# Feed-forward input projections as seven half products, in a hybrid encoder block

## The chip, the cores and the metric

One core of a Trainium2 chip runs the whole layer in one launch. The metric is the device time of the launch in microseconds, and lower is better. The core's engines have their own instruction queues: TensorE (PE in the profile) multiplies matrices into PSUM, VectorE (DVE) and ScalarE (ACT) do elementwise work, GpSimd (POOL) does elementwise work too, and SyncE (SP) starts DMA transfers.

## The reference

512 tokens, model width 1024, all in float32. The layer is: a feed-forward block, a mixer, a second feed-forward block, a final norm.

```python
x = x + 0.5 * swiglu(rms_norm(x, ffn1_norm), ffn1_w_in, ffn1_w_out)
...                      # mixer: h = rms_norm(x); P = h @ w_in; gated convolution, SSD scan, merge
x = x + 0.5 * swiglu(rms_norm(x, ffn2_norm), ffn2_w_in, ffn2_w_out)
return rms_norm(x, final_norm)

def swiglu(h, w_in, w_out):
    g, u = jnp.split(h @ w_in, 2, axis=-1)      # w_in is 1024 x 5632, two halves of 2816
    return (jax.nn.silu(g) * u) @ w_out
```

## The kernel before, in words

**Layout.** The activations are kept transposed: 128 features on the partitions, 512 tokens along the row, so the width of 1024 is 8 tiles (`KT`). The hidden width of 2816 is 22 tiles (`FT`).

**Precision.** A product in float32 is made from three products in the faster type fp32r. Each operand is split into a high part (a cast) and a low part (the rest): `wh`, `wl` for a weight block, and two halves of `xw` for an input. `mm3` (L169) issues for each of the 8 input tiles high x high, high x low and low x high, all into one PSUM bank. So a projection to 128 output features is 24 matmuls that each stream 512 columns.

**Weights.** `prep` (L110) takes the next 512 KB block from the list `src`: SyncE loads it to `wraw` (two buffers), ScalarE casts it to `wh` (L124), VectorE subtracts to get `wl` (L125). `take` (L131) hands out the oldest prepared block and starts the next `prep`; `wh` and `wl` have three buffers each.

**Feed-forward.** `ffn` (L249) loops over the 22 hidden tiles. For each it runs one projection for the gate and one for the up half, and then `hidden` (L253): VectorE multiplies both by the norm's factor per token (`tg`, `tu`), ScalarE takes SiLU (`sg`), GpSimd multiplies (`hf`, L261), and `split` makes the high and low part of the hidden tile (`hk`). Then the output projection runs over 8 output tiles `m`, 22 hidden tiles each, in three weight blocks (`kcut`), and VectorE adds half of the result to the residual (L275). The residual `xall` stays in SBUF through the whole program. In the second feed-forward block the last output tile is done in two halves of 256 tokens, with the final norm and the stores behind them (`finish`, L684).

**Order.** TensorE's instructions stand as the code issues them. `Order` (L42) counts finished input tiles (ticks), and pieces such as the norm's sums are put in when a tick is reached. The other engines' order is made by the scheduler of the tile framework; a tile is written only when its buffer's last users are done.

Of the kernel before, what the change touches and what calls it, by code (L numbers as in the profile page):

```python
# [17 lines left out]
P = 128  # L18
# [21 lines left out]


# [28 lines left out]
def hybrid_block(ctx: ExitStack, tc: tile.TileContext, xT, w1i, w1o, wmx, wz0, wso, wsso,  # L70
# [3 lines left out]
    wp = ctx.enter_context(tc.tile_pool(name="wp", bufs=3))  # L74
    act = ctx.enter_context(tc.tile_pool(name="act", bufs=1))
    tp = ctx.enter_context(tc.tile_pool(name="tp", bufs=2))
    ps = ctx.enter_context(tc.tile_pool(name="ps", bufs=1, space=bass.MemoryType.PSUM))
    ctx.enter_context(tc.manual_schedule(engines={mybir.EngineType.PE}))
# [4 lines left out]
    src += [(w1i[i], KT) for i in range(2 * FT)]  # L83
    kcut = [(0, 8), (8, 16), (16, FT)]
    fout = lambda w: [(w[m, :, a * P : b * P], b - a) for m in range(KT) for a, b in kcut]
# [19 lines left out]
    src += [(w2i[i], KT) for i in range(2 * FT)]  # L105
# [4 lines left out]
    def prep():  # L110

        if not src:
            return
        ap, _ = src.pop(0)
        n = ap.shape[-1]
        raw = wp.tile([P, D], F32, tag="wraw", name="wraw", bufs=2)
        cuts = [slice(0, n)]
        if len(src) >= NSRC - 2:
            cuts = [slice(0, n // 2), slice(n // 2, n)]
        nc.sync.dma_start(raw[:, :n], ap)  # L120
        wh = wp.tile([P, D], F32R, tag="wh", name="wh")
        wl = wp.tile([P, D], F32R, tag="wl", name="wl")
        for h in cuts:
            cast = nc.scalar.copy(wh[:, h], raw[:, h])  # L124
            nc.vector.tensor_tensor(wl[:, h], raw[:, h], wh[:, h].bitcast(F32), ALU.subtract)  # L125
        ready.append((wh, wl))
        return cast

    NSRC = len(src)

    def take():  # L131
        w = ready.pop(0)
        prep()
        return w


    xall = pers.tile([P, KT, T], F32, name="xall")
    xr = [xall[:, j, :] for j in range(KT)]
# [19 lines left out]

    warm = tp.tile([P, NC], F32, tag="ms", name="warm")
# [9 lines left out]
    def mm3(out, w, xs, first=True, last=True, tk=slice(0, T)):  # L169

        wh, wl = w
        n = len(xs)
        for i, xk in enumerate(xs):
            sl = slice(i * P, (i + 1) * P)
            nc.tensor.matmul(out, wh[:, sl], xk[:, 0, tk], start=first and i == 0, stop=False)  # L175
            nc.tensor.matmul(out, wh[:, sl], xk[:, 1, tk], start=False, stop=False)  # L176
            nc.tensor.matmul(out, wl[:, sl], xk[:, 0, tk], start=False, stop=last and i == n - 1)  # L177
            sq.tick()
# [7 lines left out]
    def split(dst, s):  # L186
        nc.scalar.copy(dst[:, 0, :], s)
        nc.vector.tensor_tensor(dst[:, 1, :], s, dst[:, 0, :].bitcast(F32), ALU.subtract)

    class Norm:  # L190
# [3 lines left out]
        def __init__(self, gain):  # L194
# [3 lines left out]
            self.xw = []  # L198

        def parts(self, j):  # L200
            xk = act.tile([P, 2, T], F32R, tag="xw", name="xw", bufs=KT)
            g = col(self.gain + j)
            nc.scalar.activation(xk[:, 0, :], xr[j], AF.Copy, scale=g)  # L203
            nc.vector.scalar_tensor_tensor(xk[:, 1, :], xr[j], g, xk[:, 0, :].bitcast(F32),  # L204
                                           ALU.mult, ALU.subtract)
            self.xw.append(xk)
# [42 lines left out]
    def ffn(nrm, nxt, tags=("mm",)):  # L249
# [3 lines left out]
        def hidden(pg, pu):  # L253
# [7 lines left out]
            nc.gpsimd.tensor_tensor(hf, sg, tu, ALU.mult)  # L261
# [4 lines left out]
        for f in range(FT):  # L266
            pg = project(xw, tags[2 * f] if 2 * f < len(tags) else "mm")
            pu = project(xw, tags[2 * f + 1] if 2 * f + 1 < len(tags) else "mm")
            sq.at(nrm.ok, lambda pg=pg, pu=pu: hidden(pg, pu))
        sq.run()  # L270
        for m in range(KT if nxt is not None else KT - 1):
            pt = bank()
            for a, b in kcut:
                mm3(pt, take(), hid[a:b], a == 0, b == FT)
            nc.vector.scalar_tensor_tensor(xr[m], pt, 0.5, xr[m], ALU.mult, ALU.add)  # L275
# [6 lines left out]
        return hid  # L282


    n1 = Norm(PF_N1)
    prep()
    for j in range(0, KT, 2):
        nc.sync.dma_start(xall[:, j : j + 2, :], xT[:, j : j + 2, :])
    keep(12, "sg", zeros("ta"))
    for j in range(KT):  # L290
        n1.parts(j)
        if j == 6:
            cast = prep()
    nc.sync.dma_start(pf[:, PF_SC:], pfeat[:, PF_SC:])
    nc.sync.dma_start(cst, csts[:, :3, :])
    mgt = tp.tile([P, P], F32, tag="td", name="mgt", bufs=3)
    nc.sync.dma_start(mgt, csts[:, 3, :])
    nc.sync.dma_start(pr, prow)

    def first_sums():  # L300
        with tc.issue_after(cast.ins):
# [3 lines left out]

    sq.at(9, first_sums)
    n1.later(22, 28)
# [475 lines left out]
```

## Time and profile before

| | |
|---|---|
| median of 3 runs | 1499.1 us (1498.96 to 1499.4) |
| profiled execution, its own time | 1499.53 us |
| span of the profiled execution | 1497.7 us |
| TensorE busy | 1486.5 us, 99% of the span |
| VectorE busy | 794.9 us, 53% |
| ScalarE busy | 604.5 us, 40% |
| GpSimd busy | 223.7 us, 15% |
| granted TensorE clock | 0.999 of full speed |
| DMA | 139.49 MB, 93 GB/s in the mean |

How to read it: in a row of the timeline stand start and duration in us, the engine, the line of the kernel, the operation, what it writes and reads, and the shape. Matmuls overlap, so the pace of TensorE is the distance from one start to the next, not the duration. In a row of a group stand count, busy time, mean duration in ns, and the idle time of the engine ahead of the group with its releaser.

### The profile page before, as it was taken

The numbers are of one execution on the slowest core, as the hardware profiler recorded it, in microseconds if no ns is written. First come the engines' busy times: TensorE is split into PE (matmuls) and PEld (weight loads), VectorE is DVE, ScalarE is ACT, GpSimd is POOL, SyncE is SP. The second block draws the span as 40 slices with busy tenths as digits, with TensorE's granted clock in tenths as the row PEclk, the third lists the DMA queues.
The fourth block names the chain that finished last, engine by engine and source line by source line (L and its number), as shares of the span: only waits on it lengthen the run. The fifth ranks groups of instructions, "written<-read, shape, count | busy, mean of one in ns | idle before, by whom it ended". The sixth has DMA issues, their size and how long they took to land.

```text
span 1497.7 us, 18035 instructions
## 1 busy us (share of the span) xinstructions
PE 1486.5 (99%) x7233; PEld 1252.9 (84%) x7234; DVE 794.9 (53%) x925; ACT 604.5 (40%) x914; POOL 223.7 (15%) x206
## 2 busy tenths in 40 slices
PE   9999999999999999999999999999999999999998
PEld 6888888888888999888888888888888888888887
DVE  6454554333687777778653256554544545453223
ACT  6233332222587777667641122222243322232222
POOL 1111111000033322212200011111121111110011
PEclk9999999999999999999999999999999999999999
DMA  5323333323312222122223333333222222223333
GB/s 194 98 86 101 96 99 92 105 89 99 93 63 67 69 77 71 58 85 71 71 81 113 93 94 98 99 99 99 96 100 86 98 99 96 101 86 104 88 106 106
DMA packets 40964, 139.49 MB, mean 93 GB/s; under 512 B 4656, under 2 KB 7088, under 8 KB 40880
## 3 DMA queue, kind: packets, MB, share of 16 engines
q1 hardware_dynamic: 40192, 137.79, 29.6%
q8 instruction: 57, 0.93, 0.3%
q10 hardware_dynamic: 688, 0.54, 0.1%
q14 instruction: 27, 0.22, 0.0%
HBM read 136.22 MB, written 2.10 MB: 92 GB/s over the span
## 4 chain that ended last, share of the span: by engine, by line
PE 96%; DVE 2%; DMA 1%; issue 0%; ACT 0%; POOL 0%; SPq 0%; POOLq 0%; ACTq 0%; DVEq 0%
PE mm L176 28%; PE mm L175 28%; PE mm L177 28%; PE mm L327 2%; PE mm L328 2%; PE mm L326 2%; PE py L514 2%; PE sg L501 1%; DVE cv L392 1%; PE po L525 1%; PE po L469 1%; DVE wl L125 0%; PE sg L425 0%; DMA xall<-xT 0%; PE tr L446 0%
## 5 line engine op out<-in xcount | busy, mean ns | idle before, releaser
L124 ACT CAST wh<-wraw 128x1024 fp32r<-128x1024 f32 (+2 forms) x262 | 269.7, 1030 | 679.4 <-PE mm L176 625.9
L175 PE MATMUL mm<-xw,wh 128*128 128x512 f32 x1256 | 500.4, 398 | 0.5 <-ACT xw L203 0.5
L125 DVE TENSOR_TENSOR wl<-wraw,wh 128x1024 fp32r<-128x1024 f32 (+2 forms) x262 | 386.0, 1474 | 213.0 <-ACT wh L124 211.9
L176 PE MATMUL mm<-xw,wh 128*128 128x512 f32 x1256 | 489.2, 389 | 0.5 <-DVE xw L204 0.5
L177 PE MATMUL mm<-xw,wl 128*128 128x512 f32 x1256 | 489.6, 390 | 0.0
L177 PEld LDWEIGHTS mm<-xw,wl 128*128 128x128 f32 x1256 | 235.7, 188 | 50.0 <-DVE wl L125 0.4
L176 PEld LDWEIGHTS mm<-xw,wh 128*128 128x128 f32 x1256 | 236.1, 188 | 48.4 <-DVE xw L204 1.2
L175 PEld LDWEIGHTS mm<-xw,wh 128*128 128x128 f32 x1256 | 235.9, 188 | 48.3 <-ACT xw L203 1.0
L175 PE MATMUL mm<-hk,wh 128*128 128x512 f32 (+1 forms) x374 | 141.0, 377 | 0.0
L176 PE MATMUL mm<-hk,wh 128*128 128x512 f32 (+1 forms) x374 | 140.8, 377 | 0.0
L177 PE MATMUL mm<-hk,wl 128*128 128x512 f32 (+1 forms) x374 | 140.8, 376 | 0.0
L261 POOL TENSOR_TENSOR hf<-sg,tu 128x512 f32<-128x512 f32 x44 | 59.5, 1353 | 400.5 <-ACT wh L124 285.1
L259 DVE TENSOR_TENSOR tu<-mm,rb 128x512 f32<-128x512 f32 x42 | 29.0, 692 | 134.2 <-PE mm L177 134.2
L177 PEld LDWEIGHTS mm<-hk,wl 128*128 128x128 f32 x374 | 70.4, 188 | 13.0
L176 PEld LDWEIGHTS mm<-hk,wh 128*128 128x128 f32 x374 | 70.4, 188 | 12.9
L175 PEld LDWEIGHTS mm<-hk,wh 128*128 128x128 f32 x374 | 70.4, 188 | 12.8
L392 DVE SCALAR_TENSOR_TENSOR cv<-xp,pf,cv 128x512 f32<-128x512 f32 x96 | 73.9, 769 | 2.6 <-ACT cv L389 1.1
L326 PE MATMUL mm<-wh,xw 128*128 128x256 f32 (+1 forms) x256 | 74.9, 293 | 0.0
L327 PE MATMUL mm<-wl,xw 128*128 128x256 f32 (+1 forms) x256 | 72.7, 284 | 0.0
L328 PE MATMUL mm<-wh,xw 128*128 128x256 f32 (+1 forms) x256 | 72.7, 284 | 0.0
L255 DVE TENSOR_TENSOR tg<-mm,rb 128x512 f32<-128x512 f32 x43 | 29.7, 692 | 66.9 <-PE mm L177 63.3
L216 POOL TENSOR_TENSOR nacc<-nacc,nsq 128x512 f32<-128x512 f32 x18 | 26.4, 1469 | 223.5 <-ACT nsq L213 223.5
(182 smaller groups left out, 1669.9 us busy)
## 6 DMA issues: line engine op xcount, KB each, us to landing
wraw<-wmx SPq DMA_DIRECT2D x86, 512.0 KB, 3.6
wraw<-w1i SPq DMA_DIRECT2D x44, 512.0 KB, 3.6
wraw<-w2i SPq DMA_DIRECT2D x44, 512.0 KB, 3.2
wraw<-w2o SPq DMA_DIRECT2D x18, 512.0 KB, 3.5
wraw<-w1o SPq DMA_DIRECT2D x16, 512.0 KB, 3.5
wraw<-wsso SPq DMA_DIRECT2D x16, 512.0 KB, 3.8
wraw<-wso SPq DMA_DIRECT2D x8, 512.0 KB, 3.2
wraw<-wmo SPq DMA_DIRECT2D x8, 512.0 KB, 3.2
```

The lines of the kernel that those rows point to most:

```text
L124: cast = nc.scalar.copy(wh[:, h], raw[:, h])
L125: nc.vector.tensor_tensor(wl[:, h], raw[:, h], wh[:, h].bitcast(F32), ALU.subtract)
L175: nc.tensor.matmul(out, wh[:, sl], xk[:, 0, tk], start=first and i == 0, stop=False)
L176: nc.tensor.matmul(out, wh[:, sl], xk[:, 1, tk], start=False, stop=False)
L177: nc.tensor.matmul(out, wl[:, sl], xk[:, 0, tk], start=False, stop=last and i == n - 1)
L255: nc.vector.tensor_tensor(tg, pg, nrm.rb, ALU.mult)
L261: nc.gpsimd.tensor_tensor(hf, sg, tu, ALU.mult)
L326: nc.tensor.matmul(o, xw[k][:, 0, tk], wh[:, sl], start=k == 0, stop=False)
L327: nc.tensor.matmul(o, xw[k][:, 0, tk], wl[:, sl], start=False, stop=False)
L328: nc.tensor.matmul(o, xw[k][:, 1, tk], wh[:, sl], start=False, stop=k == KT - 1)
L392: nc.vector.scalar_tensor_tensor(cv, xp[:, q : q + T], col(PF_CW + 4 * ft + q), cv, ALU.mult, ALU.add)
L514: nc.tensor.matmul(py[:, h, :], self.ex[c][:, h, :], self.xdt[:, c, d0 : d0 + P], start=True, stop=True)
```

## The change

**Seven half products.** For a pair (the gate tile and the up tile of one hidden tile) the two weight blocks are seen as a 2 x 2 matrix of blocks: rows are gate and up, columns are the two halves of the input width (4 input tiles each). The input is a 2 x 2 matrix too: rows are the halves of the width, columns are tokens 0 to 255 and 256 to 511. Instead of 8 block products the Strassen form (Winograd's) takes 7, with sums of blocks made ahead on both sides. Each block product is 4 input tiles x 3 fp32r products of 256 columns.

- `Norm.sums_of_x` makes the four sums of the input, once for each block, and their high and low parts (`hT`, `lT`).
- `Pair.prepare` makes the weight side: the gate's parts `gh`, `gl`; the sums `f13`, `f24` and their parts `h13`, `l13`, `h24`, `l24`; the up half's second half `a22`. The gate's low part is not a subtraction on VectorE: ScalarE writes the negated high part into `gl`, and a DMA that GpSimd starts adds the weights from DRAM to it (`accum_op`).
- `Pair.product` issues the 12 matmuls of a product, `Pair.after` the work behind it. The order of products is 1, 5, 4 of the pair before, 6, 2, 3, 7. Products 1, 6, 7 and 4 accumulate in one bank, and its intermediate states are copied out (`p1`, `p6`) or read (`ut`). Two sets of three banks alternate.
- 4 hidden tiles of the first block (`N1`) and 1 of the second (`N2`) stay plain; their projections run while the sums are made. 18 + 21 = 39 tiles go as pairs.
- The factor per token of the up half moves to the output side (`add`), where the residual is updated in two VectorE steps instead of one. The product of gate and up moves from GpSimd to VectorE. `hid` stays float32, and its split to `hk` is done in the output projection, whose first two output tiles therefore run side by side.

**Buffers.** Raw weights have three buffers of their own. All else of that size, prepared weights, inputs, hidden tiles and the residual, shares 38 slots. The residual leaves SBUF: the first block reloads the input `xT` after its pairs, stores the result to DRAM (`xs1`), and the second does so with `xs1` and `xd`. In mixer groups 0 and 1 `prep` is queued on ScalarE behind what was issued there last (`turns`).

**Order, TensorE.** In the middle of the first block's projections; `mm_...` and `py_...` are banks, and `wh`, `wl` the weight's parts. Before, one projection (its first two input tiles):

```order
L175 MATMUL mm_1027<-xw_110,wh_950 128x512
L176 MATMUL mm_1027<-xw_110,wh_950 128x512
L177 MATMUL mm_1027<-xw_110,wl_951 128x512
L175 MATMUL mm_1027<-xw_113,wh_950 128x512
L176 MATMUL mm_1027<-xw_113,wh_950 128x512
L177 MATMUL mm_1027<-xw_113,wl_951 128x512
```

Now, where product 5 of a pair ends and product 4 of the pair before begins:

```order
L433 MATMUL mm_1283<-hT_422,h13_1194 128x256
L433 MATMUL mm_1283<-lT_423,h13_1194 128x256
L433 MATMUL mm_1283<-hT_422,l13_1214 128x256
L433 MATMUL py_1153<-hT_255,a22_1135 128x256
L433 MATMUL py_1153<-lT_256,a22_1135 128x256
L433 MATMUL py_1153<-hT_255,a22_1135 128x256
L433 MATMUL py_1153<-hT_297,a22_1135 128x256
```

The rows stream 256 columns instead of 512, and a bank of the pair before is written once more inside the next pair. Over the program 1872 matmuls of 512 columns go and 3276 of 256 come; all other matmuls keep their number and shape.

**Order, VectorE.** At the same place. Before, in a hidden tile's time:

```order
L259 TENSOR_TENSOR tu_774<-mm_735,rb_297 128x512
L125 TENSOR_TENSOR wl_763<-wraw_760,wh_762 128x1024
L188 TENSOR_TENSOR hk_778<-hf_776,hk_778 128x512
L255 TENSOR_TENSOR tg_843<-mm_766,rb_297 128x512
L125 TENSOR_TENSOR wl_805<-wraw_802,wh_804 128x1024
```

Now, for one pair (`gt`, `ut`, `hid` of the pair on TensorE, the rest for the pair after the next), with `a22_1263` of 512 columns behind it:

```order
L447 TENSOR_TENSOR gt_1116<-mm_1027,p1_1040 128x256
L449 TENSOR_TENSOR gt_1116<-mm_1026,p6_1100 128x256
L450 TENSOR_TENSOR gt_1116<-gt_1116,rb_379 128x512
L456 TENSOR_TENSOR ut_1150<-mm_1025,p5_1061 128x256
L463 TENSOR_TENSOR hid_1024<-ut_1150,gt_1116 128x256
L372 TENSOR_TENSOR f13_1191<-wraw_1102 128x512
L373 TENSOR_TENSOR f13_1191<-wraw_1047,wraw_1102 128x512
L380 TENSOR_TENSOR f24_1209<-wraw_1047,f13_1191 128x512
L381 TENSOR_TENSOR f24_1209<-wraw_1047,f24_1209 128x512
L459 TENSOR_TENSOR hid_1024<-mm_1025,gt_1116 128x256
L388 TENSOR_TENSOR l13_1214<-f13_1191,h13_1194 128x1024
L388 TENSOR_TENSOR l24_1246<-f24_1209,h24_1212 128x1024
```

Five instructions became thirteen. In every second pair the rows of `f13` and `f24` stand between those of `gt` and `ut`.

**Order, ScalarE.** Before, in a hidden tile's time and the start of the next:

```order
L187 CAST hk_778<-hf_776 128x512
L124 CAST wh_804<-wraw_802 128x1024
L257 ACTIVATE sg_845<-tg_843 128x512
L124 CAST wh_835<-wraw_833 128x1024
L187 CAST hk_851<-hf_849 128x512
```

Now (`gl` is what the accumulating DMA waits for):

```order
L451 ACTIVATE gt_1116<-gt_1116 128x512
L357 ACTIVATE gl_1170<-wraw_1047 128x1024
L443 COPY p1_1168<-py_1153 128x256
L359 CAST gh_1172<-wraw_1047 128x1024
L443 COPY p5_1189<-po_1154 128x256
L375 CAST h13_1194<-f13_1191 128x1024
L383 CAST h24_1212<-f24_1209 128x1024
L443 COPY p6_1228<-py_1153 128x256
L394 CAST a22_1263<-wraw_1102 128x512
```

The copies out of the banks stand between the casts of the next weights.

The core of the diff:

```diff
+KH, TH, DH = KT // 2, T // 2, D // 2
+N1, N2 = 4, 1
+RAWS = 3
+SLOTS = 41 - RAWS
...
+        def gate_parts(self, add=True):
+            rg = self.raw[0]
+            self.gl = a4("gl", [P, D], F32R)
+            if add:
+                nc.scalar.activation(self.gl, rg, AF.Copy, scale=-1.0)
+            self.gh = a4("gh", [P, D], F32R)
+            nc.scalar.copy(self.gh, rg)
+            if add:
+                nc.gpsimd.dma_start(self.gl, self.w[2 * self.f], accum_op=ALU.add)
+            else:
+                nc.vector.tensor_tensor(self.gl, rg, self.gh.bitcast(F32), ALU.subtract)
...
+        def s13(self):
+            a11, _ = self.halves(0)
+            a21, a22 = self.halves(1)
+            self.f13 = a4("f13", [P, 2, DH])
+            nc.vector.tensor_tensor(self.f13[:, 0, :], a21, a22, ALU.add)
+            nc.vector.tensor_tensor(self.f13[:, 1, :], a11, a21, ALU.add)
+            self.h13 = a4("h13", [P, 2, DH], F32R)
+            nc.scalar.copy(self.h13, self.f13)
...
+        def product(self, n, nrm):
+            out = {1: self.a, 6: self.a, 7: self.a, 4: self.a, 5: self.c, 3: self.c, 2: self.b}[n]
+            xi = {1: 0, 2: 2, 3: 3, 5: 4, 6: 5, 7: 6, 4: 7}[n]
+            wh, wl = self.weights(n)
+            first = n in (1, 5, 2)
+            for k in range(KH):
+                xh, xl = nrm.form(xi, k)
+                sl = slice(k * P, (k + 1) * P)
+                for i, (wk, xk) in enumerate(((wh, xh), (wh, xl), (wl, xh))):
+                    nc.tensor.matmul(out, wk[:, sl], xk, start=first and k == i == 0,
+                                     stop=k == KH - 1 and i == 2, skip_group_check=True)
...
+        def after(self, n, nrm, hid):
+            lo, hi = slice(0, TH), slice(TH, T)
+            if n in (1, 5, 6):
+                t = tp.tile([P, TH], F32, tag={1: "st0", 5: "st1", 6: "st2"}[n], name="p%d" % n, bufs=1)
+                nc.scalar.copy(t, self.c if n == 5 else self.a)
+                setattr(self, "p%d" % n, t)
+            elif n == 2:
+                self.g = tp.tile([P, T], F32, tag="tc", name="gt")
+                nc.vector.tensor_tensor(self.g[:, lo], self.b, self.p1, ALU.add)
+            elif n == 3:
+                nc.vector.tensor_tensor(self.g[:, hi], self.c, self.p6, ALU.add)
+                nc.vector.tensor_tensor(self.g, self.g, nrm.rb, ALU.mult)
+                nc.scalar.activation(self.g, self.g, AF.Silu)
...
-            tu = tp.tile([P, T], F32, tag="tc", name="tu")
-            nc.vector.tensor_tensor(tu, pu, nrm.rb, ALU.mult)
-            hf = tp.tile([P, T], F32, tag="td", name="hf", bufs=3)
-            nc.gpsimd.tensor_tensor(hf, sg, tu, ALU.mult)
-            hk = act.tile([P, 2, T], F32R, tag="act", name="hk", bufs=FT)
-            split(hk, hf)
-            hid.append(hk)
...
+        for p, q in enumerate(pairs):
+            hid_tile(q.f)
+            q.banks(sets[p % 2])
+            order = (1, 5, 4, 6, 2, 3, 7) if p < len(pairs) - 1 else (1, 5, 4, 6, 2, 7, 3)
+            for step, n in enumerate(order):
+                o = prev if n == 4 else q
+                if o is not None:
+                    o.product(n, nrm)
+                    o.after(n, nrm, hid[o.f])
+                if p or step:
+                    ahead(p + 1, step)
+            prev = q
...
+            nc.vector.scalar_tensor_tensor(t[:, :n], pt, -0.5, nrm.rb[:, tk], ALU.mult, ALU.mult)
+            nc.vector.tensor_tensor(xr[m][:, tk], t[:, :n], xr[m][:, tk], ALU.add)
```

More of the change, by code (lines that the diff above doesn't have):

```diff
@@ L267, in ffn @@
+        hk = []
+        for f in range(plain):
+            hid_tile(f)
             pg = project(xw, tags[2 * f] if 2 * f < len(tags) else "mm")
+            if f == plain - 1:
+                sq.at(sq.now + 4, lambda: ahead(1, 0))
             pu = project(xw, tags[2 * f + 1] if 2 * f + 1 < len(tags) else "mm")
[L269 to L275, printed above, removed]
+            sq.at(nrm.ok, lambda f=f, pg=pg, pu=pu: hidden(f, pg, pu))
@@ L292, in hybrid_block @@
         if j == 6:
[L293 to L298, printed above, removed]
+            prep(halves=True)
     def first_sums():
-        with tc.issue_after(cast.ins):
+        with behind():
             for j in range(KT):
```

357 lines of the change are left out of this document (283 added, 74 removed).

## The prediction

> **What bounds the kernel now.** I read the page's first part and its chain of waits, then the stage table, to see whether one engine bounds every stage, and then timelines for that engine's pace.
>
> ```profile
> span 1497.7 us, 18035 instructions
> PE 96%; DVE 2%; DMA 1%; issue 0%; ACT 0%; POOL 0%; SPq 0%; POOLq 0%; ACTq 0%; DVEq 0%
> 50.00:350.00 300.00, 300.00 (x1325) 248.43 (x1324) 132.27 (x125) 86.53 (x106) 32.37 (x26) 1.00 0.33 97
> ```
>
> TensorE carries 96% of the chain. The third row is a stage inside the first feed-forward block: TensorE is busy 300.00 of 300.00 us, VectorE 132, ScalarE 87, GpSimd 32, the clock is full and the DMA engines are at 0.33. Only fewer or shorter matmuls help there, so what a matmul costs at either length decides. Starts from the timelines, at 512 columns (first and thirteenth of a run), at 256 with a new weight block each time (first and fifteenth, last output tile), and at 256 in the mixer's gates (first and ninth):
>
> ```profile
> 1462.79 0.39 PE L177 MATMUL mm<-hk,wl 128*128 128x512 f32 x1
> ...
> 1465.51 0.39 PE L177 MATMUL mm<-hk,wl 128*128 128x512 f32 x1
> 1477.73 0.28 PE L175 MATMUL mm<-hk,wh 128*128 128x256 f32 x1
> ...
> 1479.41 0.28 PE L177 MATMUL mm<-hk,wl 128*128 128x256 f32 x1
> 496.83 0.28 PE L326 MATMUL mm<-wh,xw 128*128 128x256 f32 x1
> ...
> 497.79 0.28 PE L328 MATMUL mm<-wh,xw 128*128 128x256 f32 x1
> ```
>
> 2.72 us over 12 steps is 0.2267 us; 1.68 over 14 and 0.96 over 8 are both 0.1200. The duration column (0.39 and 0.28) overstates both: matmuls overlap. A half-length matmul costs 53% of a whole one, not 50%: the line through the two points is 13.3 ns fixed and 0.417 ns a column. This eats part of what seven products for eight saves.
>
> **The projections.** A hidden tile is 48 x 0.2267 = 10.88 us now and 7 x 12 = 84 matmuls x 0.1200 = 10.08 us as a pair, 0.80 less: 1280 ns of columns saved, 36 x 13.3 = 480 ns of fixed part added. For 39 pairs that is **-31.3 us**, if nothing else sets the pair's pace.
>
> **Can VectorE follow?** It goes from five instructions to thirteen per tile. Nearest rows:
>
> ```profile
> L188 DVE TENSOR_TENSOR hk<-hf,hk 128x512 fp32r<-128x512 f32 x44 | 29.9, 679 | 5.6 <-ACT hk L187 5.6
> L479 DVE TENSOR_TENSOR st<-po,st 128x256 f32<-128x256 f32 x16 | 6.6, 415 | 0.5 <-PE po L469 0.5
> 803.66 1.23 DVE L125 TENSOR_TENSOR wl<-wraw,wh 128x1024 fp32r<-128x1024 f32 x1 [4.21 <-ACT wh L124]
> 152.35 2.35 DVE L125 TENSOR_TENSOR wl<-wraw,wh 128x1024 fp32r<-128x1024 f32 x1 [0.21 <-ACT wh L124]
> 152.31 1.32 POOL L261 TENSOR_TENSOR hf<-sg,tu 128x512 f32<-128x512 f32 x1 [9.56 <-ACT wh L124]
> ```
>
> Six of 512 columns (`f13`, `f24` twice each, `a22`, the factor on `gt`) are 6 x 0.68 = 4.08; two of 1024 (`l13`, `l24`) 2 x 1.23 = 2.46; five of 256 are 5 x 0.415 = 2.08. Sum 8.62 us, 86% of 10.08. The last two rows are the danger: the same subtraction took 2.35 instead of 1.23 us when GpSimd's multiply ran beside it. That multiply is gone; GpSimd's DMA work takes its place.
>
> ScalarE, from these rows:
>
> ```profile
> L124 ACT CAST wh<-wraw 128x1024 fp32r<-128x1024 f32 x238 | 250.6, 1053 | 614.5 <-PE mm L176 568.5 <-issue 25.2 <-PE mm L177 6.3
> L203 ACT ACTIVATE xw<-xall,pf 128x512 fp32r<-128x512 f32 x24 | 16.7, 720 | 1.6 <-DMA xall<-xT 0.8
> L257 ACT ACTIVATE sg<-tg 128x512 f32<-128x512 f32 x44 | 27.6, 626 | 0.0
> L474 ACT COPY st<-po 128x256 f32<-128x256 f32 x8 | 2.9, 364 | 0.0
> ```
>
> Three casts are 3.16, the scaled copy to `gl` between 1.05 and 2 x 0.72 = 1.44 (I take 1.25), `a22` and SiLU 0.63 each, three bank copies 1.09: 6.8 us, 67%.
>
> Both orders alternate over two pairs, so I walked two pairs through the queues, from the start of one. Its products end at 1.44, 2.88 and so on to 10.08; some 0.25 later a result can be read. VectorE: first `gt` at 7.5, second at 8.9, factor done at 10.0, `ut` waits for product 7 (10.3 to 10.8), `hid` waits for SiLU (11.2), the four sums to 14.0, the other `hid` waits for product 4 (14.7 to 15.1), `l13` 16.3, `l24` 17.5, `a22` 18.2; the second pair likewise, with `a22` at 27.1, and the third pair's first result comes at 27.6. The round closes with about 2.5 us of waiting in 20.16. The prepared weights are for the pair that begins at 20.16, and product 5 wants `l13` at about 22: 5 us early. Product 4 overwrites the bank that `ut` reads, at 13.0 and 23.0; `ut` is done at 10.8 and 21.6. The bank copies have over 1 us too. Thus VectorE's work is hidden at **0**, with one eighth of its time to spare; were the cover gone, each 0.1 us more per pair would cost 3.9 us.
>
> **The accumulating DMA** is new, and queues one GpSimd-issued transfer per pair.
>
> ```profile
> wraw<-w1i SPq DMA_DIRECT2D x44, 512.0 KB, 3.6
> xall<-xT SPq DMA_DIRECT2D x4, 512.0 KB, 6.2
> ```
>
> In the walk `gl` is written at 11.9 for a pair that starts at 20.16 and reads `gl` at its third matmul, 20.4: 8.5 us. In the other pair it is 12.2. A plain 512 KB landed in 3.6 us, four at once in 6.2. Adding means reading the destination as well, so I bound it by 3.6 and, if it moves at a quarter of that rate, 14.4; I take twice, 7.2, nearest to the row of shared engines. That fits at **0**. [...] Engine time: 0.33 of 10.88 us for two loads is 1.8 us each, so two loads and one at twice that are 7.2 of 10.08.
>
> **Edges.** *Start*: a walk through the eight plain projections (5.44 us each) gives VectorE some 45 us of work between 5 and 54 us; the last plain weights are ready 1.7 us ahead, `l13` of the first pair at 53.7, when product 1 begins, one product ahead of its use. **0**, bounds 0 to +3. *Output projections*: the first needs `hk` every 6 x 0.2267 = 1.36 us while VectorE spends 0.68 plus its share of weights; but the last pair's `hid` and two weight subtractions stand ahead of the fourth `hk`, which is ready about 0.4 us late, in both blocks: **+0.8**. *Residual and mixer*: reload and stores have tens of us; the raw loads are one buffer deeper, and `turns` delays casts in groups 0 and 1, where TensorE now loses little:
>
> ```profile
> PE sg L501 <- ACT au L488: 1.5, 1, 1.5
> PE po L525 <- DVE yo L528: 0.5, 1, 0.5
> 1487.60 0.44 DVE xall L707
> 1488.06 0.43 ACT nlast L708
> ```
>
> At best these two waits go (-2.0), at worst they double; I take **0**. *Tail*: the last two rows are pieces of the final chain. The residual update there becomes two VectorE steps (+0.42 by the 0.415 row, and a hand-over), and SyncE issues three stores instead of two: **+0.7**.
>
> **Sum.** -31.3 + 0.8 + 0.7 = -29.8. The profiled execution took 1499.53 us (span 1497.7 plus 1.8 around it), 0.4 above the median: 1499.5 - 29.8 = 1469.7, on the median's scale **1469.3**.
>
> **Rivals.**
>
> *A. VectorE sets the pace.* For it: 86%, and the 2.35 us row. If each transfer's descriptor work blocks one subtraction by 1.12 us, VectorE has 9.74 us per pair, and the wait for SiLU (0.6 to 0.7, nothing stands ahead of `hid` to fill it) makes it 10.4: 0.35 x 39 = 13.7 us back, 1483. [...] Chance 0.18, 1478 to 1497.
>
> *B. The accumulate lands late (slower).* TensorE stands at the third matmul of product 1 until `gl` has landed, with all products of the pair behind it. Past 8.5 us the first of two pairs stalls, and past 12.2 both. Two pairs save 1.6 us, so from about 10 us on the change loses. At 14.4: 5.9 + 2.2 = 8.1 per two pairs, x 19.5 = 158, 1627. For it: nothing in this trace was issued from GpSimd or added on the way. Against it: 7.2 leaves 1.3 us even in the tight pair. [...] Chance 0.13, 1502 and up.
>
> *C. Edges go better or worse.* Both mixer waits gone and no late `hk`: 1466.5, within the forecast; more than that 0.03. First pairs short of weights, pushing the time to between 1478 and 1497: 0.03.
>
> *D. No effect*: the change does not do what it says, because a product, which is only 12 matmuls long, pays for its change of bank. 0.8 us per pair over seven products, 0.11 us each, would undo the gain. Against it: in the stage row above 1325 matmuls, with a change of bank every 24, took 300 us, 0.2264 each, no more than inside a run. 0.03, 1496 to 1502.
>
> **Numbers.** Forecast 0.60, 1463 to 1478, most likely 1469.3. The range 1462 to 1492 takes in the forecast, three quarters of A and some of C, about 0.79. 0.2% is 3.0 us, about what this measurement can tell from no change. Faster (below 1496.1): 0.60 + 0.18 + 0.06 = 0.84; same 0.03; slower 0.13.
>
> **What would show it.** In the profile after: 3276 matmuls of 256 columns at 0.120 us steps, a pair every 10.08 us, and TensorE with hardly any idle time between 55 us and the output projection. Idle time ahead of them released by the DMA into `gl` means B, by VectorE's `l13`, `l24` or `ut` means A; 1024-column subtractions near 2.35 instead of 1.23 us mean that GpSimd's DMA work blocks VectorE. Landing times of `gl` give B's size. Steps above 0.12 with no wait would make the first term wrong.

## The result and the profile after

The changed kernel took **1474.39 us** (median of 4 runs, 1473.09 to 1474.82) against 1499.25 before (1498.96 to 1500.48). The ratio is 0.9831 with a 95% interval of 0.9814 to 0.9848. The prediction was 1469.3 us with a range of 1462 to 1492. So the direction and the range held. The time came down by 24.9 us, 4.9 less than the expected 29.8.

The page of the changed kernel's profiled execution (own time 1474.82 us): its span, the busy time of two engines, the chain of waits by engine, and the group of 1024-column subtractions of the pairs:

```profile
span 1472.9 us, 21580 instructions
PE 1458.9 (99%) x8637; PEld 1295.8 (88%) x8638; DVE 925.5 (63%) x1336; ACT 729.9 (50%) x1160; POOL 196.6 (13%) x209
PE 91%; DVE 3%; ACT 3%; issue 1%; DMA 1%; POOL 0%; SPq 0%; POOLq 0%; ACTq 0%; DVEq 0%
L388 DVE TENSOR_TENSOR l<-f,h 128x1024 fp32r<-128x1024 f32 x78 | 93.9, 1220 | 14.9 <-PE tr L433 7.1
```

TensorE still carries the chain. The 78 subtractions took 1.22 us each, so nothing on GpSimd slowed them. Two stretches inside the two pair stages, in the same kernel's table of windows (span of the stretch, then busy time of TensorE, weight loads, VectorE, ScalarE and GpSimd, the granted clock, the DMA share and GB/s):

```profile
60.00:240.00 180.00, 179.93 (x1480) 178.72 (x1479) 141.00 (x230) 107.54 (x162) 13.83 (x16) 1.00 0.63 164
1160.00:1340.00 180.00, 180.00 (x1498) 179.83 (x1498) 140.28 (x230) 105.43 (x159) 13.83 (x16) 1.00 0.61 157
```

TensorE is full, the clock is full, VectorE is busy 141.00 of 180 us, which is 7.9 us of a pair. All 3276 matmuls of the products are there. From the first matmul of the products to the end of the last there are 181.43 us for 18 pairs and 211.68 for 21: 10.08 us a pair in both blocks. The transfers, in the page's last part and in the view of the tile `gl` (KB each, and us from issue to landing):

```profile
wraw<-w1i SPq DMA_DIRECT2D x44, 512.0 KB, 3.8
wraw<-w2i SPq DMA_DIRECT2D x44, 512.0 KB, 4.0
gl<-w2i POOLq DMA_DIRECT2D x21, 512.0 KB, 5.6
gl<-w1i POOLq DMA_DIRECT2D x18, 512.0 KB, 5.8
...
DMA to landing us min/median/max: 5.2/5.6/8.0
```

And what TensorE waited for (us in total, times, longest):

```profile
PE sg L795 <- ACT au L782: 1.6, 1, 1.6
...
PE py L223 <- DVE lA L263: 0.8, 1, 0.8
PE py L222 <- ACT hA L262: 0.6, 1, 0.6
```

The view has eleven rows, and none is a wait of a product (`L433`). The two rows on `lA` and `hA` are new. They belong to the second block's start. Laying the first matmuls of the stages side by side shows how the change of the span (1497.7 to 1472.9) is made up:

| stage | before, us | after, us | change | expected |
|---|---|---|---|---|
| to the first projection | 6.42 | 6.78 | +0.36 | 0 |
| first block, input | 242.75 | 227.91 | -14.84 | -14.4 |
| first block, output | 119.68 | 120.07 | +0.39 | +0.4 |
| mixer, to its last output projection | 711.19 | 711.83 | +0.64 | 0 |
| the merged output projection | 43.52 | 43.57 | +0.05 | 0 |
| second block, input | 241.53 | 228.81 | **-12.72** | **-16.8** |
| second block, output, and tail | 132.64 | 133.92 | +1.28 | +1.1 |

The largest difference, 4.1 us, is in one place. The second block's one plain pair and its norm's sums took 17.13 us, from 1110.17 to 1127.30, and the product pairs behind it ran as expected. The timeline there (start, us, engine, line, operation, and in brackets the idle time before it and its releaser):

```profile
1110.20 1.93 POOL L303 TENSOR_TENSOR nacc<-nacc,nsq 128x512 f32<-128x512 f32 x1 [2.99 <-ACT nsq L300]
1110.90 1.78 DVE L263 SCALAR_TENSOR_TENSOR lA<-x,pf,hA 128x512 fp32r<-128x512 f32 x1
1112.60 0.47 DVE L277 SCALAR_TENSOR_TENSOR xf<-x,pf,b 128x256 f32<-128x256 f32 x1
...
1114.30 0.68 DVE L971 TENSOR_TENSOR x<-mm,x 128x512 f32<-128x512 f32 x1
...
1116.20 0.50 PE L222 MATMUL py<-hA,wh 128*128 128x512 f32 x1 [0.56 <-ACT hA L262]
1116.70 0.75 DVE L263 SCALAR_TENSOR_TENSOR lA<-x,pf,hA 128x512 fp32r<-128x512 f32 x1
1117.50 0.50 PE L223 MATMUL py<-lA,wh 128*128 128x512 f32 x1 [0.80 <-DVE lA L263]
```

The last merged output projection ended near 1110.2, but VectorE added its result to the residual only at 1114.30. Ahead of that stood the parts (`L263`) and the sums (`L277` to `L283`) of earlier tiles. One part was stretched to 1.78 us beside GpSimd's addition to `nacc`; the like one at 1116.70 took 0.75. So the eighth input tile came late, `hA` and `lA` both. Behind this wait the granted clock fell, as the windows show (clock in the third column from the end):

```profile
1116.00:1118.00 2.00, 1.00 (x3) 0.64 (x4) 2.00 (x3) 2.00 (x4) 0.00 (x0) 1.00 0.64 262
1118.00:1120.00 2.00, 2.00 (x8) 1.22 (x7) 2.00 (x5) 0.01 (x1) 0.00 (x0) 0.68 0.22 51
1120.00:1122.00 2.00, 2.00 (x10) 1.81 (x9) 1.02 (x3) 1.02 (x2) 0.39 (x1) 0.50 0.55 217
```

### The profile page after: what moved, and what is told of

It reads as the page before. It is cut to its first block, busy times and chain, and to the rows that moved or that the text cites. A ratio compares the mean times of both kernels' runs of the same rounds, so it can differ in the third digit from the quotient of the medians.

```text
span 1472.9 us, 21580 instructions
## 1 busy us (share of the span) xinstructions
PE 1458.9 (99%) x8637; PEld 1295.8 (88%) x8638; DVE 925.5 (63%) x1336; ACT 729.9 (50%) x1160; POOL 196.6 (13%) x209
## 4 chain that ended last, share of the span: by engine, by line
PE 91%; DVE 3%; ACT 3%; issue 1%; DMA 1%; POOL 0%; SPq 0%; POOLq 0%; ACTq 0%; DVEq 0%
PE mm L223 18%; PE mm L224 17%; PE mm L222 17%; PE mm L433 14%; PE py L433 7%; PE po L433 4%; PE tr L433 2%; PE py L808 2%; PE mm L623 2%; PE mm L624 2%; PE mm L622 2%; PE sg L795 1%; DVE wl L147 1%; PE po L763 1%; ACT wh L146 1%
## 5 line engine op out<-in xcount | busy, mean ns | idle before, releaser
L147 DVE TENSOR_TENSOR wl<-wraw,wh 128x1024 fp32r<-128x1024 f32 (+3 forms) x184 | 220.1, 1222 | 94.1 <-ACT wh L146 93.5
L146 ACT CAST wh<-wraw 128x1024 fp32r<-128x1024 f32 (+3 forms) x184 | 181.0, 1013 | 114.2 <-PE mm L223 98.4
L222 PE MATMUL mm<-xw,wh 128*128 128x512 f32 x576 | 235.5, 409 | 0.0
L224 PE MATMUL mm<-xw,wl 128*128 128x512 f32 x576 | 224.9, 390 | 0.0
L223 PE MATMUL mm<-xw,wh 128*128 128x512 f32 x576 | 224.5, 390 | 0.0
L224 PEld LDWEIGHTS mm<-xw,wl 128*128 128x128 f32 x576 | 108.1, 188 | 23.5
L223 PEld LDWEIGHTS mm<-xw,wh 128*128 128x128 f32 x576 | 108.4, 188 | 20.7
L222 PEld LDWEIGHTS mm<-xw,wh 128*128 128x128 f32 x576 | 108.3, 188 | 20.7
L388 DVE TENSOR_TENSOR l<-f,h 128x1024 fp32r<-128x1024 f32 x78 | 93.9, 1220 | 14.9 <-PE tr L433 7.1
L689 DVE SCALAR_TENSOR_TENSOR cv<-xp,pf,cv 128x512 f32<-128x512 f32 x96 | 72.5, 756 | 14.4 <-ACT cv L686 12.7
L433 PE MATMUL mm<-hT,h 128*128 128x256 f32 x240 | 68.0, 283 | 0.0
L433 PE MATMUL mm<-lT,h 128*128 128x256 f32 x240 | 67.9, 283 | 0.0
L433 PE MATMUL mm<-hT,l 128*128 128x256 f32 x240 | 67.9, 283 | 0.0
```

The source lines that it names most:

```text
L146: last["ACT"] = nc.scalar.copy(wh[:, h], raw[:, h])
L147: last["DVE"] = nc.vector.tensor_tensor(wl[:, h], raw[:, h], wh[:, h].bitcast(F32), ALU.subtract)
L222: nc.tensor.matmul(out, wh[:, sl], xh[:, tk], start=first and i == 0, stop=False)
L223: nc.tensor.matmul(out, wh[:, sl], xl[:, tk], start=False, stop=False)
L224: nc.tensor.matmul(out, wl[:, sl], xh[:, tk], start=False, stop=last and i == n - 1)
L388: nc.vector.tensor_tensor(l, f, h.bitcast(F32), ALU.subtract)
```

## The experiments

All are variants of the changed kernel. They were timed in groups with before beside them, whose medians were 1499.09 to 1499.37 us, so the groups agree to about 0.3 us. The changed kernel itself took 1473.09 to 1474.82 us in its single executions, with medians of 1474.39 and 1473.47 (e11). So a difference of under about 1.5 us to it (e1, e2, e3, e10) is read from the profiles and not from the times. Line numbers shift by a few where an edit adds lines.

### e1: two plain pairs at the second block's start

```diff
-N1, N2 = 4, 1
+N1, N2 = 4, 2
```

> Edit: the second feed-forward block begins with two plain pairs instead of one, so its first product pair starts one pair later. Theory L (the 4.1 us that the second block loses against the sum are lost ahead of the plain pair, because VectorE delivers the last of the eight input tiles late): a plain pair costs 0.80 us more than a product pair, the waits on that tile stay, so 1475.2 us, at best 0.6 less if the later waits shrink. Rival S (they are lost because the first product pair's inputs, the sums of the norm's tiles and the weights' sums, are not ready behind one plain pair): +0.8 - 4.1, so about 1471.1 us.

Measured: 1473.82 us (1473.70 to 1474.67), between the two expectations. TensorE's waits on `lA` (0.8) and `hA` (0.6) stood where they were, as theory L said, and the stretch from 1110 us to the end of the product pairs was 228.18 us. In a second execution of the changed kernel without the fall of the clock (e11) it was 227.38. So a plain pair costs 0.80 us more than a product pair, and nothing of the loss was the first product pair's inputs. In e1's profile the clock stayed at 1.00, with the same waits.

### e2: the last two input sums behind the last tile

```diff
-        else:
+        elif m < KT - 2:
             sums2(m - KH)
+        elif m == KT - 1:
+            with tc.issue_after(last["hA"].ins), tc.issue_after(last["lA"].ins):
+                sums2(m - KH - 1)
+                sums2(m - KH)
```

> Edit: the sums of the input tiles 2 and 3 (four scalar_tensor_tensor, one subtraction and two ScalarE operations each) are issued behind the last tile's two parts instead of ahead of them. Theory L (VectorE late with the last tile; half of the 4.1 us is TensorE standing, the other half the granted clock of 0.50 to 0.68 behind the waits): the last tile's lA comes some 3 us earlier, TensorE has no wait there, the clock stays at 1.00, so 3 to 4.1 us come back: 1470.3 to 1471.4 us. Rival S (the first product pair's inputs are what is late): these sums come still later, so the loss grows by 1 to 3 us: 1475.5 to 1477.5 us. Rival C (the clock falls here by itself): the waits alone come back, 1472.4 us, and the clock still shows a fall between 1118 and 1122 us.

Measured: 1473.45 us (1472.75 to 1474.54). This is not the 1470.3 to 1471.4 of theory L. The waits on the last tile did go, but others came. TensorE's waits from 1100 to 1340 us:

```profile
PE sg L322 <- POOL rt L317: 0.8, 1, 0.8
PE mm L433 <- DVE ut L456: 0.4, 1, 0.4
PE py L224 <- DVE wl L147: 0.2, 1, 0.2
```

The first is the norm's power: its input `ms` now stood behind the moved sums on VectorE. The second is of a new kind, in the middle of the product pairs: product 4 waits until `ut` has read the bank that it overwrites. The timeline of VectorE shows why `ut` was late.

```profile
1216.62 0.69 DVE L372 TENSOR_TENSOR f<-wraw 128x512 f32<-128x512 f32 x1 [2.73 <-DMA wraw<-w2i]
```

VectorE stood 2.73 us for a plain load, with `ut` four instructions behind the addition that needed it, and product 4 began 0.54 us late. That load was issued at 1209.48 us, 1.9 us behind an accumulating transfer that was on its way until 1213.01, and landed at 1216.59, 7.1 us after its issue. In this execution product 4 stood three times (0.19, 0.44 and 0.54 us above the step), in e11 once, in the first profile never. The four loads that VectorE waited for there took 6.8 to 7.1 us. Without accumulating transfers (e4) no load of a pair took over 5.5 us, and no product stood. So this is the accumulating transfer's price on its neighbours, which the prediction did not have.

### e3: matmuls of zeros in the gap

```diff
+        if m == KT - 1:
+            keep(8, "tr", warm_in)
```

> Edit: eight matmuls of zeros, 128x512 in bf16, stand on TensorE between the last merged output projection and the second block's first projection (about 1.8 us by the 0.22 us of the like matmuls at the start); nothing else moves. Theory L with the clock as a consequence of the waits: the 1.36 us of waits on the last tile are covered, the 1.8 us of filling stand in their place, and the clock stays at 1.00: +1.8 - 1.36 - 2.0 = -1.6, so 1472.8 us. Rival C (the clock falls here whatever TensorE does): +0.4, so 1474.8 us, with a granted clock of 0.50 to 0.68 again.

Measured: 1474.74 us (1474.44 to 1475.04). The clock stayed at 1.00, but it did so in e1 too, without filling, so this does not show that filling keeps it. The 1.8 us of filling were not repaid. TensorE's waits from 1100 to 1130 us:

```profile
PE sg L322 <- POOL rt L317: 0.8, 1, 0.8
PE py L223 <- DVE lA L263: 0.3, 1, 0.3
```

The wait on `lA` shrank from 0.8 to 0.3 and the one on `hA` went. The wait on the norm's power came instead, since VectorE's queue did not move.

### e4: the gate's low part on VectorE, no accumulating transfer

```diff
-            pairs[p].prepare(step)
+            pairs[p].prepare(step, add=False)
```

The same argument is given at the two other places that prepare a first pair. `prepare` with `add=False` leaves out the copy with scale -1 and the transfer, and subtracts.

> Edit: the gate weight's low part is made by one more 128x1024 subtraction on VectorE (1.22 us) in all 39 product pairs, and the copy with scale -1 on ScalarE (1.06 us) and the accumulating DMA are gone. VectorE then needs 7.9 + 1.2 = 9.1 us of the pair's 10.08. Main theory (TensorE sets the pace and VectorE has 2.2 us to spare): the step stays at 0.1200 us, the time within 1 us of 1474.4. Rival A of the prediction (VectorE sets the pace once its load nears the pair's length, since its work comes in bursts): 0.3 to 1 us a pair, 1486 to 1513 us.

Measured: 1472.08 us (1471.73 to 1472.68), faster than the changed kernel in every run. Windows, and the plain loads:

```profile
60.00:230.00 170.00, 170.00 (x1419) 170.00 (x1418) 151.97 (x236) 88.39 (x139) 0.00 (x0) 1.00 0.33 107
```

```profile
wraw<-w1i SPq DMA_DIRECT2D x44, 512.0 KB, 3.3
wraw<-w2i SPq DMA_DIRECT2D x44, 512.0 KB, 3.5
```

VectorE is busy 151.97 of 170 us, 9.0 us of a pair instead of 7.9, and TensorE loses nothing. The DMA share falls from 0.63 to 0.33 and the plain loads land in 3.3 to 3.5 us (medians) instead of 3.8 to 4.0; the slowest load of a pair takes 5.5 us instead of 6.3 to 7.1 in the executions with transfers. The tail is 0.7 us shorter. That was a surprise and is taken up at the end.

### e5: the accumulating transfer three products later

```diff
-            if add:
-                nc.scalar.activation(self.gl, rg, AF.Copy, scale=-1.0)
...
+            elif step == 3:
+                self.gate_low()
```

`gate_low` holds the copy with scale -1 and the transfer.

> Edit: the copy with scale -1 and the accumulating transfer of the gate's low part are issued three products later (at step 3 instead of step 0), some 4.3 us nearer to their use; the number of instructions is the same. Theory (a transfer added on the way takes 5.6 to 5.8 us from issue to landing, so the tight pair of two, with 8.5 us, has 2.8 us to spare and the other 6.5): 4.3 us later the tight pair waits about 1.5 us and the other not, 19.5 x 1.5 = 29, so about 1503 us, and TensorE's waits stand at the third matmul of product 1, released by the transfer. Rival (the landing is not what product 1 waits for, the budget is wider): within 1 us of 1474.4. Should the transfers run alone and land in their shortest 5.2 us: 19.5 x 1.0 = 20, 1494 us.

Measured: 1655.02 us (1646.24 to 1663.54), six times the expected loss. TensorE's first four waits:

```profile
PE py L433 <- DMA gl<-w2i: 37.0, 10, 8.6
PE py L433 <- DMA gl<-w1i: 31.6, 9, 6.5
PE mm L433 <- DMA gl<-w1i: 31.5, 8, 5.7
PE mm L433 <- DMA gl<-w2i: 27.1, 10, 5.3
```

The place is the one named, the third matmul of product 1. But both pairs of two stood, 37 times, 3.4 us each, 127 us in all. The transfers landed in 7.1 to 8.3 us (medians) instead of 5.6 to 5.8. Issued later, a transfer holds the raw gate weights longer and meets other plain loads; that this made it slower is likely but not shown apart. The profiled execution is 186.7 us longer than the changed kernel's, and the remaining 60 us lie in the pair stages too: there the clock fell 28 times and stood at half for 147 us, part of it while TensorE waited. Around one of the waits:

```profile
1227.00:1236.00 9.00, 0.48 (x5) 0.27 (x3) 6.18 (x11) 2.32 (x3) 0.43 (x1) 0.69 0.67 175
1236.00:1238.00 2.00, 1.93 (x9) 1.93 (x10) 0.00 (x0) 0.00 (x0) 0.00 (x0) 0.50 0.00 0
1240.00:1242.00 2.00, 2.00 (x16) 2.00 (x15) 1.23 (x1) 0.91 (x2) 0.00 (x0) 0.82 0.00 0
```

So rival B of the prediction was real in its place and worse in its price. The changed kernel is kept from it by the 2.8 us between a budget of 8.4 and a landing of 5.6. Near the end of each block one budget is only 6.6 us; the transfer there landed in 5.2 to 5.3, with 1.3 us to spare.

### e6: e4 and e2 together, the norm's spread later

```diff
-    n2.later(9, 15)
+    n2.later(9, 20)
```

> Edits: the low part on VectorE as in e4, the sums of the input tiles 2 and 3 behind the last tile's parts as in e2, and the norm's spread five groups of matmuls later (20 instead of 15). Theory: e2 took 1.5 us of the waits on the last tile away, and gave it back in a wait of 0.8 on the norm's power and in 1.4 us of pairs whose weights came late beside the accumulating transfers. Without these transfers, and with the spread behind the power, the 1.5 us stay saved: 1472.1 - 1.5 = 1470.6 us. Rival (VectorE is behind by a whole tile there, so whatever goes ahead pushes something else back, the first pair's input sums here): 1471.8 to 1472.5 us, with new waits in the first pair's products 5, 6 and 7.

Measured: **1471.37 us** (1471.28 to 1471.63), the fastest kernel of the study, and between the two expectations. The ratio to before is 0.9815, with an interval of 0.9801 to 0.9828. The three waits of e2 are gone. One is new, in the second product pair (waits from 1100 to 1140 us):

```profile
PE po L433 <- DVE l L388: 1.4, 1, 1.4
PE py L223 <- DVE lA L263: 0.2, 1, 0.2
```

### e7 and e10: more work for VectorE, 1.22 us and half of it

e7 is e4 with `l13` made twice; e10 repeats 512 of its 1024 columns.

```diff
                 self.low(13)
+                nc.vector.tensor_tensor(self.l13, self.f13, self.h13.bitcast(F32), ALU.subtract)
```

> Edit: on top of e4, one subtraction of 128x1024 of each pair is done twice on VectorE (same inputs, same output). By the rows of e4 VectorE is busy 159.63 of 180 us in the first pair stage, 8.94 us of a pair; with 1.22 more it would be 10.16 of 10.08. Theory (VectorE is then the bound, rival A's condition): at least 0.1 us a pair, and with the wait for SiLU of 0.1 to 0.2 and the hand-overs 0.2 to 0.6 us: 39 x 0.2 to 0.6 = 8 to 23, so 1480 to 1495 us. Rival (the records overlap by some 0.05 us each, so VectorE has more to spare than they show): the step stays at 0.1200 us, 1472 to 1474 us.

> Edit: e4 with half of e7's extra work, one subtraction of 128x512 of each pair done twice on VectorE (0.68 us in its row). VectorE then needs some 9.6 us of the pair's 10.08. Rule P (a pair lasts as long as VectorE's work plus 0.65 to 0.8 us in which it must wait, for SiLU and for TensorE's results; e7 gave 10.79 for 10.0 to 10.16 of work): 10.25 to 10.4 us a pair, 39 x 0.17 to 0.32 = 7 to 12.5 us, 1479 to 1484.5. Rival (the waits are filled while VectorE's work is under the pair's length, only what exceeds it counts): 1472 us, a step of 0.1200 us.

Measured: e7 1500.90 us (1500.68 to 1501.82), e10 1473.59 (1473.24 to 1473.80). The same windows of e7 and then of e10, and between them e7's waits in the first block:

```profile
60.00:230.00 170.00, 161.85 (x1311) 158.01 (x1310) 156.97 (x236) 82.85 (x126) 0.00 (x0) 1.00 0.30 97
```

```profile
PE mm L434 <- DVE l L406: 7.0, 8, 0.9
PE mm L434 <- DVE ut L457: 0.4, 1, 0.4
```

```profile
60.00:230.00 170.00, 169.58 (x1412) 169.28 (x1411) 158.67 (x251) 87.34 (x136) 0.00 (x0) 1.00 0.33 106
```

The pairs of e7 took 10.82 and 10.77 us (first and second block), those of e10 10.13 and 10.08. VectorE was busy 156.97/170 x 10.82 = 10.0 us of e7's pair, with 0.8 us in which it could do nothing, and 158.67/170 x 10.13 = 9.45 of e10's, with 0.7. e7's work of 10.0 us is under the pair's 10.08, where the rival of e10 expects no loss, and yet its pair grew. So rule P holds there, with 0.7 to 0.8 us of waiting that is not filled: VectorE sets the pace once its work passes about 10.08 - 0.7 = 9.4 us. The expectation for e10 missed by its input: the repeated 512 columns added 0.4 us of busy time and not 0.68. e10 stands at the edge (0.05 us a pair lost in the first block, nothing in the second), so it alone would not decide between the two. 9.0 of e4 is below the edge, and 7.9 of the changed kernel far below.

### e8: all pairs plain, the rest of the change kept

```diff
-N1, N2 = 4, 1
+N1, N2 = 22, 22
```

Along with it go the calls that load and prepare product pairs and the sums of the input tiles.

> Edit: both blocks' inputs as 22 plain pairs, everything else of the change kept (raw weights in three buffers of their own, residual in DRAM, order of the output weights, tail). The sums of the input tiles are not made. Theory (the seven products give 31.3 us, and what the change costs elsewhere is small): before, plus 0.35 for each first output projection, 0.57 for the tail's residual in two steps, 0.64 in the mixer, less 0.37 since only 8 transfers are issued from GpSimd and its closing drain is short: about 1500.8 us, 1500.3 to 1501.5. Rival (the rest of the change costs several us, which the products cover): 1503 us or more. Rival (the rest gains): below 1499.

Measured: 1499.59 us (1499.28 to 1500.29), just under the expected range and 0.5 above before. The mixer took 407.03 us up to its `yh` products (406.55 before). The first output projection took 119.68, as before, so the 0.35 us of a late `hk` belongs to the product pairs and not to the order of the weights. So loads in three buffers, the residual in DRAM and the tail cost about half a microsecond together, and the products with what comes along with them give 1499.59 - 1474.39 = 25.2 us of their 31.3.

### e9: e6 with two plain pairs

The edit of e1, on e6.

> Edit: e6 with two plain pairs at the start of the second block instead of one. Theory (what VectorE is behind at that start, e6 shows last in a wait of 1.4 us of the second product pair on a subtraction of its weights; one more plain pair is 0.80 us dearer and leaves VectorE some 9 us to catch up): 1471.4 + 0.8 - 1.6 = 1470.6 us, and no wait of TensorE in product pairs. Rival (the wait only moves to a later pair): 1472.2 us.

Measured: 1474.87 us (1473.08 to 1475.01), a miss of both. The wait in the product pairs went, but with the sums between them the second plain pair's own weights were late (waits from 1105 to 1140 us):

```profile
PE mm L222 <- ACT wh L146: 1.3, 1, 1.3
PE mm L224 <- DVE wl L147: 0.7, 1, 0.7
```

These two waits stand close together, and behind them, from 1125.69 to 1129.10 us, the clock was at half again.

### e11: the changed kernel once more

No edit.

> Edit: none, the changed kernel itself, on the same chip and in the same call as e9, and for a second profile of it. Theory (the fall of the granted clock behind the waits at the second block's start comes in some executions only): times between 1473.0 and 1474.9 us as before, and if the profile shows 1.00 between 1110 and 1130 us, a span about 1.7 us under the first one's 1472.9. Rival (the waits bring it in every execution): the profile shows 0.50 to 0.68 there again and the span is 1472.5 to 1473.3.

Measured: 1473.47 us (1473.32 to 1473.95). The profile has the same two waits, 0.6 on `hA` and 0.8 on `lA`, and behind them a full clock:

```profile
1118.00:1120.00 2.00, 1.90 (x11) 1.16 (x10) 2.00 (x5) 0.09 (x1) 0.00 (x0) 1.00 0.18 35
1120.00:1122.00 2.00, 2.00 (x13) 1.72 (x12) 1.00 (x4) 0.94 (x1) 0.87 (x1) 1.00 0.74 236
```

The span is 1471.6 us. The stretch up to the first product took 15.70 us instead of 17.13. So 1.4 us of the 4.1 are the clock, and come in some executions. The other 2.7 are TensorE standing and starting again, and came in every profile that kept this order of VectorE's work (2.4 to 2.7 in e1, e4 and e11).

### e12: e6 with the plain pair's hidden tile later

```diff
-    n2.later(9, 20)
+    n2.later(9, 17)
+    n2.ok += 5
```

> Edit: e6 with the norm's spread at 17 instead of 20, and the plain pair's hidden tile 5 steps behind it instead of at once. In e6 VectorE stood 1.8 and 1.6 us with that tile's two instructions at its head, waiting for the copied norm and for SiLU, with the second product pair's weights queued behind them, and TensorE then waited 1.4 us on these weights. Theory (that order, not the amount of VectorE's work, makes e6's last wait): VectorE makes the weights in that time, TensorE's wait in the second product pair goes, 1471.4 - 1.5 = 1469.9 us. Rival (VectorE is behind by its amount of work): the wait moves to the product pair's other weights or to its hidden tile, 1471.0 to 1471.8 us.

Measured: 1473.66 us (1473.52 to 1473.88), 2.3 us slower than e6. VectorE's queue was served as intended, and the wait moved to ScalarE: the copy `p` that empties product 1's bank stood there behind a cast that had waited 2.75 us for VectorE's weight sums. TensorE's first wait in the second block, and windows:

```profile
PE mm L433 <- ACT p L443: 2.1, 1, 2.1
```

```profile
1126.00:1128.00 2.00, 0.17 (x2) 0.00 (x0) 1.66 (x3) 1.55 (x3) 0.00 (x0) 1.00 0.00 0
1130.00:1132.00 2.00, 2.00 (x12) 2.00 (x11) 0.55 (x1) 1.99 (x4) 0.00 (x0) 0.50 0.25 102
```

Four orders of this start (after, e2, e6, e12) lose 1.7 to 4.1 us against the expected length of that block's input, in four different places. Each edit moved the wait to what VectorE's or ScalarE's queue then served last. An order without a wait was not found, and it is open whether there is one.

## Why the prediction was right, and where it missed

**The projections** (-31.3): right. A pair takes 10.08 us in both blocks, 39 of them, with the step of 0.1200 us through seven changes of bank. Rival D (a price for each change of bank) is out. A plain pair against a product pair measured 0.80 us directly (e1 against e11).

**Can VectorE follow**: right in its answer, hidden at 0. Its work is 7.9 us by the windows and not 8.62, since neighbouring records overlap (by 0.08 us in the median of the first block's pair stage, with rows of 0.68 us that begin 0.60 us apart). The subtractions took 1.22 us, so the stretch to 2.35 that fed rival A was the multiply and not GpSimd's transfers. The deciding point of rival A is now measured: about 9.4 us of work a pair (e10), and 0.7 us a pair are lost at 10.0 (e7). Of the walk's 2.5 us of waiting per two pairs, 1.4 to 1.7 were not filled.

**The accumulating DMA**: right in its place and budgets, wrong in what else it costs. From its issue to the third matmul of product 1 the trace shows 8.4 and 12.2 us in turn, where the walk gave 8.5 and 12.2. It landed in 5.6 to 5.8 us, between the bounds of 3.6 and 14.4 and below the 7.2 taken. In the two windows of the pair stages VectorE ran nothing but `tensor_tensor`, and the slowest of the 39 transfers landed in 8.0 us. The prediction priced only the lateness of `gl`. It did not price the plain loads beside it (median 3.8 to 4.0 against 3.3 to 3.5 without, now and then late enough for a product to stand 0.2 to 0.5 us), nor what the transfers do to the tail. e4, which leaves the transfer away and lets VectorE do the work, is 1.4 to 2.3 us faster. The cheaper place for that work was the engine with time to spare.

**Edges, start**: this is the step that failed. It said 0, bounds 0 to +3, "a walk through the eight plain projections", and that is the first block's start. There it held: the products began at 53.26 us without a wait. The second block starts with one plain pair behind a projection whose results VectorE must first add, split and sum, and no walk was made there. It lost 4.1 us in the profiled execution, over the upper bound of 3: 2.7 us of TensorE standing and 1.4 of clock. In e11, with a full clock, the same place lost 2.7 us, inside the bound; the walk had missed it all the same. e2 shows that the last tile's waits go when VectorE's sums stand behind that tile, so their place in VectorE's queue was the cause of these waits. What share GpSimd's addition had in them, by the row that it stretched, no run shows apart.

**Edges, output projections** (+0.8): right, +0.39 in the first block and 0.35 in the second. **Mixer** (0, bounds -2.0 to +2.0): +0.64, and +0.48 without any products (e8). **Tail** (+0.7): +0.93, made up otherwise. The residual in two steps and its hand-over cost 0.57 ahead of the last matmul. Behind it 0.36 came, by GpSimd's closing instruction and not by the third store.

The sum of these differences against the forecast (0.36 - 0.44 + 0.64 + 0.05 + 4.1 + 0.2 = 4.9) is, to rounding, the 5.0 us by which the span missed its expected change of -29.8. The first of them is partly chance: up to the first projection the profiles of the variants took 6.45 to 6.96 us.

## What to carry to other kernels

Walk the order through the engines at every place where the pattern begins, not only where it repeats or where it begins first: here 39 pairs took 10.08 us each as computed, and one unwalked start took a seventh of the expected gain. Here the transfer that took work off VectorE did not pay, since VectorE had time to spare: without it the kernel was 1.4 to 2.3 us faster (e4). So first ask how much work the helper engine can take, which here was the pair's length less the waits that were not filled, 10.08 - 0.7 = 9.4 us. And the hidden transfer did not lose gently past its slack of 2.8 us: moved 4.3 us, it cost 181 (e5).

## What the runs showed of the hardware

**Short waits halved the clock, and it changed on a grid of 3.413 us.** In the changed kernel's first profile, e9 and e12 the steps of TensorE went to half rate for 3.41 us (in e12 from 1129.85 to 1133.26 us): 0.4265 us for 512 columns and 0.2133 for 256, exactly in proportion, without the 13.3 ns of the full rate. By these steps a stretch costs 1.5 to 1.6 us; 1.4 were measured between the changed kernel's two profiles. It followed waits of 2.1 us in one piece (e12), of 1.3 and 0.7 us close together (e9), and of 0.6 and 0.8 us close together in one execution of the changed kernel but not in another (e11), nor in e1, e4 and e10. It did not follow a single wait of 1.4 us (e6), nor the mixer's wait of 1.6 us (`sg` on `au`) in that same first profile.

The traces record the start and the length of every stretch at one clock. In all 14 profiles the time between two changes is a whole number of 3.413 us (436 of them before, 326, 1 and 102 in the changed kernel's first profile): one such window at half clock in the three profiles above, one to three in the 28 falls of e5. Cut into these windows, TensorE had stood for 1.87 us or more in the window ahead of 30 of the 31 falls inside the kernels, and no window with that much left a full clock full (the most that did was 1.86 us, in e5). So what went with a fall in these runs was how much of a wait fell into one window: a wait of 3.34 us in e5, split evenly over two, brought no fall. The 31st fall is that of the changed kernel's first profile, with 1.37 us in its window. e1, e4 and e10 had the same two waits in one window, with 1.35 to 1.36 us, and no fall. What made the difference there is open. (Behind each kernel's last matmuls the clock falls once more, after a window with 1.75 us or more of standing.)

**GpSimd's closing instruction grew with the transfers it had issued.** GpSimd's sequence ends with a drain, which begins as its last two multiplications do. Its length by the trace's record of it, and what is left of the span from the start of the last matmul:

| kernel | transfers issued from GpSimd | closing drain, us | start of the last matmul to the end, us |
|---|---|---|---|
| before | 0 | 1.51 | 6.59 |
| e4, e6, e7, e9, e10, e12 | 8 | 2.18 to 2.19 | 6.20 to 6.22 |
| e8 | 8 | 2.18 | 6.41 |
| e1 | 46 | 5.29 | 6.86 |
| after, e2, e3, e5, e11 | 47 | 5.36 to 5.37 | 6.92 to 6.94 |

In these profiles each transfer added 0.082 us: (5.37 - 2.18) / 39, and the rows with 0 and 46 lie on that line. In the changed kernel this drain ends 6.15 us after the last matmul starts, 0.7 us behind everything else, and sets the end. With 8 transfers it ends 3.0 us after that start, long before SyncE's own last drain at 5.5 (e4), and sets nothing. It is a price of the accumulating transfers that no row of the loop shows.
